# An encoder trunk's gated MLP: where the chained weight additions and the sums of activations stand in VectorE's order

## The chip, the cores and the metric

The kernel runs on one core of one Trainium2 chip. The metric is the device time of one execution in microseconds (us), the median of the runs shown. The engines are called as the profile calls them: PE (TensorE's matmuls) and PEld (its weight loads), DVE (VectorE), ACT (ScalarE), POOL (GpSimd) and SP (SyncE, which here only issues DMAs).

## The reference

Two encoder layers over 256 positions of width 2048, in float32. Each layer is a mixer (layer 0: pooling and grouped-query attention; layer 1: a bidirectional mLSTM) followed by a gated MLP, and the change touches the MLP alone:

```python
def conv_ffn(x, w_up, conv_w, conv_b, w_down):
    u = x @ w_up                       # 2048 -> 2 * 5632
    up = jnp.pad(u, ((0, 0), (1, 1), (0, 0)))
    c = conv_w.astype(u.dtype)
    u = c[0] * up[:, :-2] + c[1] * up[:, 1:-1] + c[2] * up[:, 2:] + conv_b.astype(u.dtype)
    gate, val = jnp.split(u, 2, axis=-1)
    return (jax.nn.silu(gate) * val) @ w_down    # 5632 -> 2048

for layer in range(DEPTH):             # DEPTH = 2
    ...
    x = x + mixed
    x = x + conv_ffn(rms_norm(x, norm_ffn[layer]), w_up[layer], conv_w[layer], conv_b[layer], w_down[layer])
```

## The kernel before, in words

**Precision and the weight stream.** A float32 product is made of three matmuls: every operand is split into a high part (a copy rounded to the type fp32r) and a low part (the operand less its high part), and high by high, high by low and low by high are added up in PSUM. The weights come as a stream of chunks of 128 x 1024 float32 (512 KB), in the order in which PE uses them (class `Stream`). SP loads a chunk into one of six buffers `w`, five chunks ahead. `split` then makes its two parts in `hl` (four buffers): ACT copies the high part (L127), DVE subtracts to get the low part (L128). It is called two chunks ahead of the chunk that PE is on: when PE's instructions for chunk i are written down, chunk i + 2 is split.

**What sets the order.** PE's instructions run in the order written. Those of the other engines are ordered when the program is built, by a planner with a timeline of its own: an instruction may be put ahead of earlier written ones where the plan says that its inputs are there. On the chip each engine then takes its instructions in that fixed order and waits where an input is late. Two means bind the planner: a dependence without a wait (it fixes the order of two instructions of one engine), and `keep_in_program_order`, which puts an instruction behind the one that was last written down for its engine. Work that is to be written down between matmuls is a generator in the queue of `Weave`: PE's loops call `tick` with an estimate of the time that they took, and when a task's time has come its next step is written down; `yield 1.2` asks for 1.2 us until the next step; `until` runs the tasks on until a condition holds.

**The MLP.** The 44 pairs of hidden tiles (128 gate channels with their 128 value channels) are worked off in slabs of 4, 8, 8, 8, 8, 8 (`FCH`). `up(c, f, gt, i)` makes one hidden tile of slab c: 64 matmuls over four chunks (PSUM tile `up`), then the row norm, the convolution, SiLU and the product on ACT and DVE (L419 to L992). Two neighbouring hidden tiles are a pair j, and their float32 results lie in one tile `s` of `quads`. The down-projection of a slab runs while the next slab's tiles are made. Most of it is made by blocks of two by two (two hidden tiles by two halves of the positions by two column blocks) with seven products in place of eight, which needs sums of weight blocks and sums of activation blocks. For each pair j of a slab and each half h of the output columns there is a unit A (four products into PSUM tiles `pp`, two chunks) and a unit B (three products, a chunk and a half).

**The sums of weights.** For h = 0 they are made ahead of time by DMAs in DRAM (`premix`). For h = 1 they are made on the way. The first chunk of unit A is a `Sum`: SP loads one summand into a buffer `sum` (three buffers) and POOL issues a DMA that adds the other (L112, L113). The second chunk is a `Chain`: it is loaded plainly, and then DVE adds the first half of the sum to its first half (L123), and that to its second half (L124), before it is split. So the four chunks of two units A are Sum, Chain, Sum, Chain.

**The sums of activations.** `combine(c, j)` makes four sums of the blocks of pair j: DVE L998 (two subtractions in one instruction), L999 and L1000, then ACT's copies (L1004) and DVE's subtractions (L1005) split them into `s3` (three sums, read by units A; one buffer for each j) and `s1` (read by units B; two buffers for each j).

**Rows.** `_ffn_plan` writes the order. A row is one hidden tile of slab c and, behind it, what it carries of slab c - 1. Where a slab's both halves are made by seven products (slabs 2 to 4 of layer 0, 1 to 4 of layer 1, seven in all), the eight rows of the next slab carry: rows 0 and 1 units A of h = 1 (pairs 0 and 1, then 2 and 3), rows 2 and 3 units B of h = 1, rows 4 and 5 units A of h = 0, rows 6 and 7 units B of h = 0. Behind a finished group of units its PSUM tiles are added into `x` or `acc` by four steps of `drain` (L1061), spread over the next row. The `mix` entry of pair j of slab c stands behind row max(2j + 1, last row that reads the old `s3` of j): rows 4, 4, 5 and 7 in these slabs.

Of the kernel before, what the change touches and what calls it, by code (L numbers as in the profile page):

```python
# [9 lines left out]
F32 = mybir.dt.float32  # L10
F32R = mybir.dt.float32r
# [5 lines left out]
P = 128  # L17
# [15 lines left out]
FCH = [4, 8, 8, 8, 8, 8]  # L33
# [4 lines left out]
WARM = 5  # L38
ATT_PARTS = [[4 + h for h in range(8)], [0, 1, 2, 3], [4 + h for h in range(8, 12)]]
ML_PARTS = [list(range(12)), list(range(12, 16))]  # L40

NG = 4 * KT
NB = D // 512
# [22 lines left out]
class Sum:  # L66


    def __init__(self, one, other):
        self.one, self.other = one, other  # L70
# [15 lines left out]
class Stream:  # L86


    def __init__(self, nc, wpool, spool, srcs, load_ahead, split_ahead):
        self.nc, self.wpool, self.spool, self.srcs = nc, wpool, spool, srcs  # L90
        self.la, self.sa = load_ahead, split_ahead
        self.w, self.hl = {}, {}
        self.n_load = self.n_split = self.at = 0

    def load(self, pieces=1):
# [20 lines left out]
    def split(self, then=None):  # L116
        i = self.n_split
        w, n, width = self.w.pop(i)
        if isinstance(self.srcs[i], Sum):
            self.sum = w  # L120
        elif isinstance(self.srcs[i], Chain):
            half = CH * P // 2
            self.nc.vector.tensor_add(w[:, :half], w[:, :half], self.sum[:, :half])  # L123
            self.nc.vector.tensor_add(w[:, half:], w[:, half:], w[:, :half])  # L124
        hl = self.spool.tile([P, 2, CH * P], F32R, tag="hl", name=f"hl{i}")
        for c in range(0, width, n):
            (self.nc.vector.tensor_copy if i + c == 0 else self.nc.scalar.copy)(hl[:, 0, c : c + n], w[:, c : c + n])  # L127
            self.nc.vector.tensor_sub(hl[:, 1, c : c + n], w[:, c : c + n], hl[:, 0, c : c + n].bitcast(F32))  # L128
            then and then(c // n)
        self.hl[i] = hl  # L130
        self.n_split += 1
# [76 lines left out]
def trunk(ctx: ExitStack, tc: tile.TileContext, gx, xT, xn, call, catt, cml, weights, mixes, out):  # L208
    nc = tc.nc
# [8 lines left out]
    wp = pool("wraw", 6)  # L218
# [8 lines left out]
    gcol = cp.tile([P, NG], F32, tag="gcol", name="gcol")  # L227
    a_x = actp.tile([P, KT, S], F32, tag="B1", name="xT")
    x = xp.tile([P, 2, D], F32, tag="x", name="x")
    st = Stream(nc, wp, sp, weights, 5, 2)  # L230

    gx0 = actp.tile([P, NG + 2 * S], F32, tag="B0", name="gx0")
    ctx.enter_context(tc.manual_schedule(engines={mybir.EngineType.PE}))
# [11 lines left out]
    wv = Weave()  # L245
# [708 lines left out]
    def ffn_layer(layer, norm, nxt):  # L954
        with ExitStack() as es:
# [16 lines left out]
            def up(c, f, gt, i):  # L972
# [11 lines left out]
                v.tensor_add(y[:, :, 1:S], y[:, :, 1:S], z[:, 0, :, 0 : S - 1])  # L984
                v.tensor_add(y[:, :, 0 : S - 1], y[:, :, 0 : S - 1], z[:, 1, :, 1:S])
                if i % 2 == 0:
                    quads[c, i // 2] = tp.tile([P, 4, P], F32, tag="silu", bufs=3, name=f"s{layer}_{f}")
                s_ = quads[c, i // 2][:, i % 2 * 2 : i % 2 * 2 + 2].rearrange("p a b -> p (a b)")
                a.activation(s_, y[:, 0, :], AF.Silu)
# [1 line left out]
                a.copy(gt[:, i, 0, :], s_)  # L991
                v.tensor_sub(gt[:, i, 1, :], s_, gt[:, i, 0, :].bitcast(F32))  # L992

            def combine(c, j):

                g4 = quads.pop((c, j))
                sf = sm1.tile([P, 512], F32, tag="sq", name=f"sf{layer}_{c}_{j}").rearrange("p (a b) -> p a b", a=4)
                v.tensor_sub(sf[:, 0:2], g4[:, 0::3], g4[:, 1:2].to_broadcast([P, 2, P]))  # L998
                v.tensor_add(sf[:, 2], sf[:, 1], g4[:, 0])  # L999
                v.tensor_sub(sf[:, 3], sf[:, 2], g4[:, 2])  # L1000
                s3 = kp.tile([P, 2, 3, P], F32R, tag=f"s3{j}", name=f"s3{layer}_{c}_{j}")
                s1 = st.sums.tile([P, 2, P], F32R, tag=f"s1{j}", name=f"s1{layer}_{c}_{j}")
                for d, e in ((s3, sf[:, 0:3]), (s1, sf[:, 3])):
                    a.copy(d[:, 0], e)  # L1004
                    v.tensor_sub(d[:, 1], e, d[:, 0].bitcast(F32))  # L1005
                combos[c, j] = s3, s1

            def product(ps, xs, wh, wl, first, last):
                xh, xl = xs
# [5 lines left out]
            def unit(kind, c, h, js):  # L1015
# [3 lines left out]
                if js[0] == 0:  # L1019
                    wv.until(lambda: "busy" not in pss)  # L1020
                    for e in order:
                        pss[e] = psp.tile([P, 512], F32, tag="ps", name=f"pp{layer}_{c}_{h}{e}")
                gt = gts[c]

                def part(j, k, t):
# [118 lines left out]
            for kind, c, i, *j in _ffn_plan(layer):  # L1144
                if kind == "up":
                    if i == 0:
                        gts.append(actp.tile([P, 8, 2, S], F32R, tag=f"B{c % 2}", name=f"g{layer}_{c}"))
                    up(c, f, gts[c], i)
                    f += 1
                elif kind == "down":  # L1150
                    down(c, i)
                elif kind == "two":
                    down_two(c)
                elif kind == "mix":
                    combine(c, i)
                else:
                    unit(kind, c, i, *j)

# [65 lines left out]
def _ffn_plan(layer):  # L1224
# [6 lines left out]
    for c, n in enumerate(FCH):  # L1231
# [5 lines left out]
        else:  # L1237
            slots = [[(kind, c - 1, 1, (j,))] for kind in "AB" for j in range(pairs)]
            for b in range(2 if pairs else 0):
                slots[(b + 1) * pairs // 2 - 1].append(("down", c - 1, b))  # L1240

        busy = {j: k for k, slot in enumerate(slots) for u in slot if u[0] == "A" for j in u[3]}
        for i in range(n):
            seq.append(("up", c, i))
            seq += slots[i] if i < len(slots) else []
            if c < len(FCH) - 1:
                seq += [("mix", c, j) for j in range(n // 2) if i == max(2 * j + 1, busy.get(j, 0))]
    return seq + [("two", len(FCH) - 1, 0)] + [("down", len(FCH) - 1, b) for b in range(2, NB)]


# [154 lines left out]
```

## Time and profile before

| | us |
|---|---|
| median of 3 runs | 2175.67 (2175.55 to 2177.23) |
| the profiled execution | 2172.38 |
| span of its trace | 2170.4 |

| engine | busy us | share of the span |
|---|---|---|
| PE | 2160.9 | 100% |
| PEld | 1845.4 | 85% |
| DVE | 1729.7 | 80% |
| ACT | 1406.7 | 65% |
| POOL | 128.7 | 6% |

The granted clock of PE is 1.00 in all stretches that are shown. The span runs from the first to the last instruction of the program. Busy time is the time in which at least one instruction of the engine was running; a view by windows gives it for a stretch of the span, with the number of instructions in brackets, the granted clock, the mean busy share of the 16 DMA engines and what they moved in GB/s. In a timeline the first column is the start in us from the span's start, the second the time that the line covers, and a bracket at the end names idle time of the engine ahead of the instruction and what ended it. The duration of a single instruction includes its tail, which overlaps the next one's beginning: what an instruction costs its engine is the distance to the next start.

### The profile page before, as it was taken

Reading aid. Unit: us, or ns where it says so; the run is one execution under the profiler, and the core shown is the slowest. Engines: PE = TensorE matmul, PEld = TensorE weight load, DVE = VectorE, ACT = ScalarE, POOL = GpSimd, SP = SyncE. Lnnn points to the kernel's source line nnn. Section 1 sums busy time; section 2 is a strip of 40 time slices with the busy share of each in tenths; the row PEclk is TensorE's granted clock in tenths of the full one; section 3 lists DMA queues with packets and bytes.
Section 4 is the critical chain, followed back from the end, with each engine's and each line's share of the span. In section 5 each row is a group of like instructions: output and inputs, shape, how many; then the busy total and the mean of one; then the engine's idle time right before and its main releaser. Section 6 shows DMA issues by size and latency. Waiting matters only on the chain.

```text
span 2170.4 us, 31559 instructions
## 1 busy us (share of the span) xinstructions
PE 2160.9 (100%) x11424; PEld 1845.4 (85%) x11424; DVE 1729.7 (80%) x2428; ACT 1406.7 (65%) x2200; POOL 128.7 (6%) x160
## 2 busy tenths in 40 slices
PE   9999999999999999999999999999999999999999
PEld 7888888888888888889888888888888888888887
DVE  7686678887988888976777676667888898988896
ACT  7665576766677767666554554457676777776763
POOL 0011010000000000000000010110000000000000
PEclk9999999999999999999999999999999999999999
DMA  9668988787988877757688888998978787887774
GB/s 326 220 204 255 287 247 263 231 268 243 293 272 278 281 247 234 253 193 226 203 250 248 252 243 243 276 274 249 270 214 283 253 272 248 264 266 242 233 252 163
DMA packets 157790, 543.72 MB, mean 251 GB/s; under 512 B 17498, under 2 KB 19842, under 8 KB 157634
## 3 DMA queue, kind: packets, MB, share of 16 engines
q1 hardware_dynamic: 129056, 460.10, 61.1%
q0 software_dynamic: 17440, 48.51, 13.5%
q10 hardware_dynamic: 11138, 33.11, 4.6%
q8 instruction: 89, 1.46, 0.3%
q14 instruction: 67, 0.55, 0.1%
HBM read 539.50 MB, written 60.86 MB: 277 GB/s over the span
## 4 chain that ended last, share of the span: by engine, by line
PE 92%; DVE 4%; DMA 3%; issue 1%; ACT 1%; DVEq 0%; ACTq 0%; POOLq 0%
PE up L256 40%; PE pp L256 11%; PE op L256 8%; PE dn L256 6%; PE mv L256 4%; PE mq L256 4%; PE mk L256 4%; PE mo L256 4%; PE qproj L256 3%; DVE hl L128 2%; DMA w<-in_dn 1%; PE kproj L256 1%; PE vproj L256 1%; DMA sum<-in_dn 1%; PE pool L256 1%
## 5 line engine op out<-in xcount | busy, mean ns | idle before, releaser
L128 DVE TENSOR_TENSOR hl<-w,hl 128x1024 fp32r<-128x1024 f32 (+2 forms) x836 | 1002.8, 1211 | 223.3 <-ACT hl L127 220.6
L127 ACT CAST hl<-w 128x1024 fp32r<-128x1024 f32 (+2 forms) x835 | 857.2, 1043 | 450.5 <-PE up L256 134.3
L256 PE MATMUL up<-xx,hl 128*128 128x512 f32 (+1 forms) x5632 | 996.6, 337 | 3.2 <-DVE hl L128 3.0
L256 PEld LDWEIGHTS up<-xx,hl 128*128 128x128 f32 x5632 | 865.9, 188 | 137.9 <-DVE hl L128 7.9
L256 PE MATMUL pp<-hl,s 128*128 128x512 f32 x768 | 193.2, 393 | 0.4 <-DVE hl L128 0.4
L256 PEld LDWEIGHTS pp<-hl,s 128*128 128x128 f32 x768 | 141.3, 188 | 30.2 <-DVE hl L128 1.6
L256 PE MATMUL pp<-hl,g 128*128 128x512 f32 x576 | 147.9, 391 | 0.0
L419 ACT COPY tb_up<-up 128x512 f32<-128x512 f32 x88 | 51.6, 586 | 113.0 <-PE up L256 112.8
L256 PEld LDWEIGHTS pp<-hl,g 128*128 128x128 f32 x576 | 105.4, 188 | 20.7
L256 PE MATMUL dn<-hl,g 128*128 128x512 f32 x528 | 122.7, 390 | 0.0
L256 PEld LDWEIGHTS dn<-hl,g 128*128 128x128 f32 x528 | 98.7, 188 | 20.3
L983 ACT ACTIVATE y<-tb_up,cst 128x256 f32<-128x256 f32 x176 | 103.6, 589 | 0.0
L984 DVE TENSOR_TENSOR y<-y,z 128x510 f32<-128x510 f32 x88 | 60.5, 688 | 50.2 <-ACT y L983 50.2
L981 ACT ACTIVATE z<-tb_up,cst 128x256 f32<-128x256 f32 x176 | 88.4, 502 | 7.9 <-DVE tb_up L976 6.4
L256 PE MATMUL mk<-xx,hl 128*128 128x512 f32 (+1 forms) x512 | 92.1, 337 | 0.0
L256 PE MATMUL mq<-xx,hl 128*128 128x512 f32 (+1 forms) x512 | 92.1, 337 | 0.0
L256 PE MATMUL mv<-hl,xx 128*128 128x512 f32 (+2 forms) x480 | 91.7, 350 | 0.0
L256 PE MATMUL op<-hl,cat 128*128 128x512 f32 x384 | 91.6, 393 | 0.0
L420 DVE TENSOR_TENSOR tb_up<-up,tb_up 128x512 f32<-128x512 f32 x88 | 60.6, 688 | 38.4 <-ACT tb_up L419 38.4
L256 PE MATMUL mo<-hl,xx 128*128 128x512 f32 x384 | 90.5, 391 | 0.0
L256 PE MATMUL op<-hl,mcat 128*128 128x512 f32 x384 | 89.5, 392 | 0.0
L256 PEld LDWEIGHTS mq<-xx,hl 128*128 128x128 f32 x512 | 79.2, 188 | 11.6
(232 smaller groups left out, 2097.0 us busy)
## 6 DMA issues: line engine op xcount, KB each, us to landing
w<-in_up SPq DMA_DIRECT2D x352, 512.0 KB, 4.8
w<-in_dn SPq DMA_DIRECT2D x176, 512.0 KB, 4.5
w<-in_m_in SPq DMA_DIRECT2D x124, 512.0 KB, 5.3
m<-in_dn ACTq DMA_DIRECT2D x56, 512.0 KB, 6.0
w<-m SPq DMA_DIRECT2D x56, 512.0 KB, 4.8
w<-in_a_in SPq DMA_DIRECT2D x46, 512.0 KB, 4.8
sum<-in_dn SPq DMA_DIRECT2D x36, 512.0 KB, 4.9
sum<-in_dn POOLq DMA_DIRECT2D x36, 512.0 KB, 8.9
```

The source lines that it names most:

```text
L127: (self.nc.vector.tensor_copy if i + c == 0 else self.nc.scalar.copy)(hl[:, 0, c : c + n], w[:, c : c + n])
L128: self.nc.vector.tensor_sub(hl[:, 1, c : c + n], w[:, c : c + n], hl[:, 0, c : c + n].bitcast(F32))
L256: last_mm[0] = pe.matmul(out_, lhsT, rhs, start=start, stop=stop, skip_group_check=True)
L419: a.copy(tb, ps[:, :, 1, :])
L420: v.tensor_add(tb, ps[:, :, 0, :], tb)
L981: a.activation(z[:, 0, j, :], u[:, j, :], AF.Copy, scale=cw(tl, 0))
L983: a.activation(y[:, j, :], u[:, j, :], AF.Identity, scale=cw(tl, 1), bias=cw(tl, 3))
L984: v.tensor_add(y[:, :, 1:S], y[:, :, 1:S], z[:, 0, :, 0 : S - 1])
```

## The change

It has two parts, both in the order of work; no instruction's operands or sizes change.

In `Stream`, the first addition of a Chain chunk (L123) gets an order behind the low part of the chunk that stands two places ahead of it in the stream. The order has no wait on a semaphore, as both are on DVE. `lows` holds the two last low parts written down.

`combine` becomes a generator that makes the sums of several pairs one after the other, is queued in `Weave`, and has its DVE instructions pinned behind what was written down for DVE before. A table `MIX` says in which row it is queued: pair 0 of slab c behind row 4 of that slab, pairs 1 and 2 behind row 6, pair 3 behind row 0 of the next slab, the last with a delay of 6.0 us, the others with 0.6 (slab 0, with two pairs: rows 1 and 3). `unit` runs the queue until its pairs' sums are written down, and `up` does so until fewer than three of the tiles `s` are still to be read.

```diff
--- before.py
+++ after.py
@@ -39,6 +39,11 @@
 ATT_PARTS = [[4 + h for h in range(8)], [0, 1, 2, 3], [4 + h for h in range(8, 12)]]
 ML_PARTS = [list(range(12)), list(range(12, 16))]
 
+
+MIX = {(0, 1): [(0, [0])], (0, 3): [(0, [1])]}
+for _c in range(1, len(FCH) - 1):
+    MIX.update({(_c, 4): [(_c, [0])], (_c, 6): [(_c, [1, 2])], (_c + 1, 0): [(_c, [3])]})
+
 NG = 4 * KT
 NB = D // 512
 
@@ -86,10 +91,10 @@
 class Stream:
 
 
-    def __init__(self, nc, wpool, spool, srcs, load_ahead, split_ahead):
-        self.nc, self.wpool, self.spool, self.srcs = nc, wpool, spool, srcs
+    def __init__(self, nc, behind, wpool, spool, srcs, load_ahead, split_ahead):
+        self.nc, self.behind, self.wpool, self.spool, self.srcs = nc, behind, wpool, spool, srcs
         self.la, self.sa = load_ahead, split_ahead
-        self.w, self.hl = {}, {}
+        self.w, self.hl, self.lows = {}, {}, []
         self.n_load = self.n_split = self.at = 0
 
     def load(self, pieces=1):
@@ -120,12 +125,14 @@
             self.sum = w
         elif isinstance(self.srcs[i], Chain):
             half = CH * P // 2
-            self.nc.vector.tensor_add(w[:, :half], w[:, :half], self.sum[:, :half])
+            self.behind(self.nc.vector.tensor_add(w[:, :half], w[:, :half], self.sum[:, :half]), self.lows[0])
             self.nc.vector.tensor_add(w[:, half:], w[:, half:], w[:, :half])
         hl = self.spool.tile([P, 2, CH * P], F32R, tag="hl", name=f"hl{i}")
         for c in range(0, width, n):
             (self.nc.vector.tensor_copy if i + c == 0 else self.nc.scalar.copy)(hl[:, 0, c : c + n], w[:, c : c + n])
-            self.nc.vector.tensor_sub(hl[:, 1, c : c + n], w[:, c : c + n], hl[:, 0, c : c + n].bitcast(F32))
+            low = self.nc.vector.tensor_sub(
+                hl[:, 1, c : c + n], w[:, c : c + n], hl[:, 0, c : c + n].bitcast(F32))
+            self.lows = self.lows[-1:] + [low]
             then and then(c // n)
         self.hl[i] = hl
         self.n_split += 1
@@ -227,7 +234,13 @@
     gcol = cp.tile([P, NG], F32, tag="gcol", name="gcol")
     a_x = actp.tile([P, KT, S], F32, tag="B1", name="xT")
     x = xp.tile([P, 2, D], F32, tag="x", name="x")
-    st = Stream(nc, wp, sp, weights, 5, 2)
+    order = mybir.DependencyInfo(mybir.DependencyClass.NoSync, mybir.DependencyReason.SCHED_ONLY)
+
+    def behind(ins, other):
+
+        tc.add_manual_dep(ins.ins, other.ins.name, order, reason="order")
+
+    st = Stream(nc, behind, wp, sp, weights, 5, 2)
 
     gx0 = actp.tile([P, NG + 2 * S], F32, tag="B0", name="gx0")
     ctx.enter_context(tc.manual_schedule(engines={mybir.EngineType.PE}))
@@ -984,6 +997,7 @@
                 v.tensor_add(y[:, :, 1:S], y[:, :, 1:S], z[:, 0, :, 0 : S - 1])
                 v.tensor_add(y[:, :, 0 : S - 1], y[:, :, 0 : S - 1], z[:, 1, :, 1:S])
                 if i % 2 == 0:
+                    wv.until(lambda: sum(e < len(FCH) - 1 for e, _ in quads) < 3)
                     quads[c, i // 2] = tp.tile([P, 4, P], F32, tag="silu", bufs=3, name=f"s{layer}_{f}")
                 s_ = quads[c, i // 2][:, i % 2 * 2 : i % 2 * 2 + 2].rearrange("p a b -> p (a b)")
                 a.activation(s_, y[:, 0, :], AF.Silu)
@@ -991,19 +1005,28 @@
                 a.copy(gt[:, i, 0, :], s_)
                 v.tensor_sub(gt[:, i, 1, :], s_, gt[:, i, 0, :].bitcast(F32))
 
-            def combine(c, j):
-
-                g4 = quads.pop((c, j))
-                sf = sm1.tile([P, 512], F32, tag="sq", name=f"sf{layer}_{c}_{j}").rearrange("p (a b) -> p a b", a=4)
-                v.tensor_sub(sf[:, 0:2], g4[:, 0::3], g4[:, 1:2].to_broadcast([P, 2, P]))
-                v.tensor_add(sf[:, 2], sf[:, 1], g4[:, 0])
-                v.tensor_sub(sf[:, 3], sf[:, 2], g4[:, 2])
-                s3 = kp.tile([P, 2, 3, P], F32R, tag=f"s3{j}", name=f"s3{layer}_{c}_{j}")
-                s1 = st.sums.tile([P, 2, P], F32R, tag=f"s1{j}", name=f"s1{layer}_{c}_{j}")
-                for d, e in ((s3, sf[:, 0:3]), (s1, sf[:, 3])):
-                    a.copy(d[:, 0], e)
-                    v.tensor_sub(d[:, 1], e, d[:, 0].bitcast(F32))
-                combos[c, j] = s3, s1
+            def combine(c, js):
+
+                pin = tc.keep_in_program_order
+                for j in js:
+                    g4 = quads[c, j]
+                    sf = sm1.tile([P, 512], F32, tag="sq", name=f"sf{layer}_{c}_{j}").rearrange(
+                        "p (a b) -> p a b", a=4)
+                    pin(v.tensor_sub(sf[:, 0:2], g4[:, 0::3], g4[:, 1:2].to_broadcast([P, 2, P])))
+                    yield 0.9
+                    pin(v.tensor_add(sf[:, 2], sf[:, 1], g4[:, 0]))
+                    pin(v.tensor_sub(sf[:, 3], sf[:, 2], g4[:, 2]))
+                    yield 1.2
+                    s3 = kp.tile([P, 2, 3, P], F32R, tag=f"s3{j}", name=f"s3{layer}_{c}_{j}")
+                    s1 = st.sums.tile([P, 2, P], F32R, tag=f"s1{j}", name=f"s1{layer}_{c}_{j}")
+                    for d, e in ((s3, sf[:, 0:3]), (s1, sf[:, 3])):
+                        a.copy(d[:, 0], e)
+                    yield 1.2
+                    for d, e in ((s3, sf[:, 0:3]), (s1, sf[:, 3])):
+                        pin(v.tensor_sub(d[:, 1], e, d[:, 0].bitcast(F32)))
+                        yield 0.6
+                    del quads[c, j]
+                    combos[c, j] = s3, s1
 
             def product(ps, xs, wh, wl, first, last):
                 xh, xl = xs
@@ -1020,6 +1043,7 @@
                     wv.until(lambda: "busy" not in pss)
                     for e in order:
                         pss[e] = psp.tile([P, 512], F32, tag="ps", name=f"pp{layer}_{c}_{h}{e}")
+                wv.until(lambda: all((c, j) in combos for j in js))
                 gt = gts[c]
 
                 def part(j, k, t):
@@ -1152,7 +1176,7 @@
                 elif kind == "two":
                     down_two(c)
                 elif kind == "mix":
-                    combine(c, i)
+                    wv.add(combine(c, i), 6.0 if 3 in i else 0.6)
                 else:
                     unit(kind, c, i, *j)
 
@@ -1238,13 +1262,10 @@
             slots = [[(kind, c - 1, 1, (j,))] for kind in "AB" for j in range(pairs)]
             for b in range(2 if pairs else 0):
                 slots[(b + 1) * pairs // 2 - 1].append(("down", c - 1, b))
-
-        busy = {j: k for k, slot in enumerate(slots) for u in slot if u[0] == "A" for j in u[3]}
         for i in range(n):
             seq.append(("up", c, i))
             seq += slots[i] if i < len(slots) else []
-            if c < len(FCH) - 1:
-                seq += [("mix", c, j) for j in range(n // 2) if i == max(2 * j + 1, busy.get(j, 0))]
+            seq += [("mix", *e) for e in MIX.get((c, i), ())]
     return seq + [("two", len(FCH) - 1, 0)] + [("down", len(FCH) - 1, b) for b in range(2, NB)]
```

## The prediction

> **What bounds the kernel now.** I read the page's first part, then the waits of PE, then windows cut where PE starts a new slab.
>
> ```profile
> PE 2160.9 (100%) x11424; PEld 1845.4 (85%) x11424; DVE 1729.7 (80%) x2428; ACT 1406.7 (65%) x2200; POOL 128.7 (6%) x160
> PE up L256 <- DVE hl L128: 3.0, 6, 0.7
> PE pp L256 <- DVE hl L128: 0.4, 1, 0.4
> ```
>
> PE sets the time, and no matmul is added or taken away. So the change can only give back what PE loses by waiting. In the MLP that is seven waits, all for the low part of a weight chunk (L128). What a wait shows as idle is less than it costs, because the two matmuls before the one that waits are stretched too. So I take the cost from lengths: one window for each of the seven slabs' rows, and windows of single rows of one of them.
>
> ```profile
> 542.84:671.25 128.41, 128.00 (x681) 109.13 (x680) 113.52 (x152) 94.78 (x144) 6.71 (x8) 1.00 0.86 281
> 671.25:801.36 130.11, 128.87 (x681) 108.90 (x680) 115.42 (x154) 92.45 (x141) 6.78 (x8) 1.00 0.86 273
> 801.36:929.46 128.10, 128.06 (x682) 109.44 (x682) 115.00 (x143) 91.23 (x137) 1.19 (x2) 1.00 0.72 238
> 1609.20:1737.06 127.86, 127.81 (x682) 109.23 (x681) 109.31 (x145) 94.36 (x145) 3.44 (x4) 1.00 0.81 261
> 1737.06:1866.46 129.40, 128.34 (x681) 109.09 (x681) 114.93 (x154) 92.65 (x140) 3.41 (x4) 1.00 0.81 260
> 1866.46:1994.91 128.45, 127.84 (x681) 109.22 (x680) 115.78 (x154) 93.12 (x141) 3.44 (x4) 1.00 0.81 262
> 1994.91:2123.23 128.32, 128.07 (x682) 109.44 (x681) 115.17 (x143) 91.31 (x137) 0.85 (x1) 1.00 0.72 238
> sum 900.65, PE 896.99 PEld 764.46 DVE 799.12 ACT 649.90 POOL 25.83; mean PE 128.14 PEld 109.21 DVE 114.16 ACT 92.84 POOL 3.69
> ```
>
> The columns are the stretch, its length, then busy PE, PEld, DVE, ACT and POOL. The rows of the slab from 1866.46 on, with the last row before it:
>
> ```profile
> 1851.22:1866.46 15.24, 15.24 (x83) 13.11 (x82) 11.67 (x17) 11.07 (x17) 0.00 (x0) 1.00 0.74 240
> 1866.46:1883.97 17.51, 16.90 (x89) 14.16 (x88) 17.51 (x24) 12.18 (x18) 0.85 (x1) 1.00 0.70 220
> 1883.97:1900.62 16.65, 16.65 (x89) 14.18 (x88) 16.07 (x23) 12.83 (x22) 1.73 (x2) 1.00 1.01 328
> 1900.62:1915.86 15.24, 15.24 (x83) 13.10 (x82) 14.39 (x21) 10.50 (x15) 0.87 (x1) 1.00 1.00 313
> 1947.76:1964.43 16.67, 16.67 (x89) 14.23 (x88) 13.82 (x20) 12.71 (x22) 0.00 (x0) 1.00 0.73 250
> ```
>
> These are row 7 of the slab before, then rows 0, 1, 2 and 5. A row with units A takes 16.67 us where nothing waits, one with units B 15.24, so eight rows take 4 x 16.67 + 4 x 15.24 = 127.64 and seven slabs 893.48. They took 900.65. **7.17 us, 0.33% of the time, is all that can come back there.** Row 0 alone lost 17.51 - 16.67 = 0.84, with DVE busy throughout; in row 7 just before it DVE had 15.24 - 11.67 = 3.57 us free. The timeline of DVE across that border says why (the last two lines are PE's):
>
> ```profile
> 1860.85 1.23 DVE L128 TENSOR_TENSOR hl<-w,hl 128x1024 fp32r<-128x1024 f32 x1 [1.22 <-ACT hl L127]
> 1864.00 0.69 DVE L123 TENSOR_TENSOR w<-w,sum 128x512 f32<-128x512 f32 x1 [1.59 <-DMA w<-in_dn]
> 1864.61 0.68 DVE L420 TENSOR_TENSOR tb_up<-up,tb_up 128x512 f32<-128x512 f32 x1
> 1865.21 0.68 DVE L124 TENSOR_TENSOR w<-w 128x512 f32<-128x512 f32 x1
> 1866.41 1.22 DVE L128 TENSOR_TENSOR hl<-w,hl 128x1024 fp32r<-128x1024 f32 x1
> 1866.46 0.39 PE L256 MATMUL up<-xx,hl 128*128 128x512 f32 x1
> 1867.68 10.96 PE L256 MATMUL up<-xx,hl 128*128 128x256 f32 x62 [0.61 <-DVE hl L128]
> ```
>
> The low part of row 0's first chunk starts at 1866.41, just when PE wants it. Before it stands the addition of a Chain chunk that PE needs five chunks later. DVE waited 1.59 us for that chunk's load, with everything behind it, and then spent two additions of 0.60 (start to start). The low part would have been ready some 2.8 us sooner.
>
> **The change, part by part.** *Chained additions.* There are 36 Chain chunks, and L123's waits for loads are
>
> ```profile
> L123 DVE TENSOR_TENSOR w<-w,sum x36: 677/692/694, 298.3 to 2015.9; 128x512 f32<-128x512 f32 x36
> DVE w L123 <- DMA w<-in_dn: 26.2, 17, 2.9
> DVE w L123 <- DMA sum<-in_dn: 4.2, 2, 2.3
> ```
>
> 30.4 us of DVE in 19 waits. By the new order the first addition of the Chain in place 6 stands behind the low part of place 4, and that of place 8 behind place 6. It then runs after the low parts which PE needs first, and its load, asked for five chunks ahead, has had three more chunks' time (2.8 us each) to land. So I count these waits as gone. Nothing is added to DVE's work. Two costs are new. If the additions stand next to each other, the second must wait for the first's end, 0.68, instead of starting at 0.60. And ACT's copy of the chunk, about 1.0, must come between them and the chunk's low part; the low part of the chunk between (1.14) covers it. Without that cover DVE idles 1.0 for each Chain, 2.0 in each of rows 0 and 1.
>
> The dependent neighbours in the trace cost a bit more than the tail:
>
> ```profile
> 1789.50 0.68 DVE L984 TENSOR_TENSOR y<-y,z 128x510 f32<-128x510 f32 x1
> 1790.21 0.69 DVE L985 TENSOR_TENSOR y<-y,z 128x510 f32<-128x510 f32 x1
> ```
>
> 0.71 from start to start against 0.60, so 0.11 a Chain, 0.22 a row: covered by the lead that the waits give back. The Trainium skill ("VectorE: DVE Perf Modes", The DRAIN you can't avoid) says that a semaphore between chained DVE operations costs nothing extra, since the next one waits for an empty pipe anyway; by it the 0.11 would be 0. This trace disagrees for additions, by that 0.71.
>
> How much of the 7.17 hangs on these waits? Not all of it:
>
> ```profile
> 721.43:737.59 16.16, 15.63 (x83) 13.14 (x84) 14.31 (x19) 13.36 (x23) 0.00 (x0) 1.00 0.85 311
> 1786.77:1802.73 15.96, 15.59 (x84) 13.11 (x83) 14.07 (x19) 12.38 (x21) 0.00 (x0) 1.00 0.76 261
> 1782.39 1.05 ACT L127 CAST hl<-w 128x1024 fp32r<-128x1024 f32 x1 [2.73 <-DMA w<-in_dn]
> ```
>
> Two rows 3 lost 0.92 and 0.72. There ACT itself waits for a load: in rows 1 and 2 the DMA engines are full (1.01 and 1.00 above), with the sums' loads and additions in them. Leaving out 0.4 for the row before the first of them, that is 2.0 us of late loads, and 7.17 - 2.0 = **5.2 us for the early additions**. For the late loads the bounds are 0 (the DMA share stays) and 2.0 (DVE, less behind, frees its buffers earlier); I take 0.7, nearer to nothing, because the same bytes must move.
>
> *The sums of activations.* 36 pairs, each with three DVE sums, two ACT copies and two DVE low parts; no DMA is issued.
>
> ```profile
> L1005 DVE TENSOR_TENSOR s<-sf,s x72: 279/420/554, 295.2 to 2018.7; 128x384 fp32r<-128x384 f32 x36, 128x128 fp32r<-128x128 f32 x36
> L998 DVE TENSOR_TENSOR sf<-s x36: 408/417/425, 291.5 to 2008.2; 128x256 f32<-128x256 f32 x36
> L999 DVE TENSOR_TENSOR sf<-sf,s x36: 278/283/291, 292.2 to 2010.3; 128x128 f32<-128x128 f32 x36
> ```
>
> With L1000 like L999 a pair costs DVE at most 0.42 + 0.28 + 0.28 + 0.84 = 1.8 us, or 1.4 with the tails of 0.08 taken off. The work is the same; its place is not. Pair 0 goes into row 5, pairs 1 and 2 into row 7. Row 5 has 16.67 - 13.82 = 2.85 us free and gives up pair 1. Row 7 takes about 2.8, less what it held of pair 2, and gives up the wait and the two additions; with 3.57 free it holds that, and nothing waits for these pairs before the next slab. The tile `s` of pair 1 is kept until row 7, with pairs 0 and 2 beside it three in all, and pair 0's is free again in row 5, before row 6 asks for one. Slab 0's pairs keep their rows, and `until` issues nothing. Cost: 0; without that room, up to 2.8 in row 7 of seven slabs. Pair 3 is the tight one. Its sums are now written down 6 us into row 1, behind the low part of the first of the four chunks of the units A that follow, and its own low parts behind that of the second. PE reads its `s3` with the third:
>
> ```profile
> 1888.67 0.55 DVE L1005 TENSOR_TENSOR s<-sf,s 128x384 fp32r<-128x384 f32 x1
> 1894.56 1.22 DVE L128 TENSOR_TENSOR hl<-sum,hl 128x1024 fp32r<-128x1024 f32 x1
> 1897.88 2.22 PE L256 MATMUL pp<-hl,s 128*128 128x512 f32 x9
> ```
>
> Before, `s3` was there at 1889.2, 8.7 us ahead of its use at 1897.88. The low part at 1894.56 is that of the third chunk, so that of the second ends at about 1894.6; behind it `s3` comes at some 1895.5: 2.4 us to spare. Queued behind these on DVE are the low parts of the third and fourth chunks, and PE waits for those next. Bounds: 0, and the whole 1.4 in each of seven rows, 9.9. As the lead in that row is about 2 us (the low part of 1894.56 ends 2.1 before its use) and grows by what row 0 no longer wastes, I take 0.1 a slab, 0.7.
>
> **Sum:** -5.2 - 0.7 + 0.7 = -5.2 us on the profiled execution's 2172.38, so 2167.2. The median of the runs is 3.29 above it; by the same difference 2175.67 - 5.2 = **2170.5**. For this way of going alone: -7.2 to -3.0, 2168.5 to 2172.7.
>
> **The rivals.** (a) *The wait moves into pair 3's sums: slower.* The pinned instructions meet a DVE that has no lead; the late chunks of row 1, or `s3` itself, come 1.4 us late in seven rows: +9.9 - 5.2 = +4.7, 2180.4. It decides from 5.2 / 7 = 0.74 a row. For it: in row 1 DVE is busy 16.07 of 16.65. Against: pair 3's sums stood in rows 0 and 1 before too, so the two rows' work is the same but for the additions from row 7. (b) *Row 0 stays short of DVE.* Its work is at least the 17.51 of now, plus the two additions that stood before it, against 16.67; if the lead that row 7 leaves is used up, about half of the 5.2 is lost again: 2173.1. Against: row 7's free time and the 1.59 make a lead of some 3 us, more than the 2.0 that row 0 lacks. (c) *The change does nothing to the stalls:* the planner puts other early work there, and loads decide: 2175.5. Against: in the row 0 shown DVE's only wait for a load is L123's, and the order forbids that place to it.
>
> **How the numbers follow.** Forecast 0.60, (a) 0.17, (b) 0.15, (c) 0.08. A difference of 0.2%, 4.35 us, is about what a measurement can tell from none. The forecast is beyond it in five cases of six (0.50), and the tail of (b) adds 0.02: faster 0.52. Slower is (a) and a little of (c): 0.18. The rest, 0.30, lies within. The range goes from the cap, 7.2 off (2168.5), up to 2178.5: it holds (b), (c) and the milder part of (a).
>
> **What would show it.** Right: no wait of L123 for a DMA; slabs of 127.6 to 128.0 us; row 0 at 16.7, and first chunks of a slab no longer late. Rows 3 with late loads may stay. Wrong: PE waits for ACT or DVE of `s` (L1004, L1005) or for L128 in row 1; a longer wait of L128 for ACT's copy than before in rows 0 and 1; slabs over 128.7 us.

## The result, and the profile after

| | before | after |
|---|---|---|
| median of the runs, us | 2175.66 (2175.55 to 2177.23) | 2189.3 (2188.71 to 2190.35) |
| the profiled execution, us | 2172.38 | 2188.71 |
| span of its trace, us | 2170.4 | 2186.6 |

The changed kernel takes 1.0062 times as long [1.0044, 1.0079]: **13.6 us slower, where 5.2 us faster was forecast**. The time lies outside the range. The granted clock is 1.00 in all stretches that this section shows, as before.

The first part of the page after, to be held against that of before (PE 2160.9 us, DVE 1729.7):

```profile
PE 2165.9 (99%) x11424; PEld 1845.7 (84%) x11424; DVE 1735.1 (79%) x2428; ACT 1404.8 (64%) x2200; POOL 128.5 (6%) x160
```

The counts of instructions are the same. Two lines of the waits of PE stand in the place of the seven waits for L128 (columns: us in total, times, longest; the low part is now L133 and ACT's high part L132):

```profile
PE pp L269 <- DVE hl L133: 11.1, 12, 1.1
PE pp L269 <- ACT hl L132: 3.2, 11, 0.6
```

PE no longer waits before `up`, at the head of a slab, but before `pp`, in the units. The first addition of a Chain chunk (now L128) has no wait for a load left in 36 instructions, where 30.4 us stood; its row among the groups of instructions of the kernel after (busy us, mean ns, idle time before it):

```profile
L128 DVE TENSOR_TENSOR w<-w,sum 128x512 f32<-128x512 f32 x36 | 24.6, 684 | 0.0
```

So the wait that the change was to remove is removed, and the time went elsewhere. The windows of the same seven slabs (the stretch, its length, then busy PE, PEld, DVE, ACT, POOL), with three of them left out, of 131.57, 131.83 and 131.59 us:

```profile
542.96:673.64 130.68, 128.76 (x682) 109.14 (x680) 114.57 (x151) 93.93 (x146) 6.71 (x8) 1.00 0.87 278
...
1616.54:1744.53 127.99, 127.93 (x682) 109.30 (x681) 111.85 (x148) 93.97 (x147) 3.43 (x4) 1.00 0.82 260
...
1876.12:2007.68 131.56, 128.99 (x681) 109.12 (x680) 116.28 (x153) 92.39 (x141) 3.44 (x4) 1.00 0.79 256
2007.68:2139.52 131.84, 129.26 (x682) 109.33 (x681) 116.17 (x145) 91.55 (x138) 0.85 (x1) 1.00 0.72 232
sum 917.06, PE 902.14 PEld 764.45 DVE 807.40 ACT 648.39 POOL 25.81; mean PE 128.88 PEld 109.21 DVE 115.34 ACT 92.63 POOL 3.69
```

917.06 - 900.65 = 16.41 us, all of the 16.33 by which the two profiled executions differ. Six slabs lose 3.0 to 4.2 us against the 127.64 of rows without a wait; the fourth loses 0.35. Cut by rows, around the slab that the prediction showed, and with row 0 of the fourth slab as the last line:

```profile
1860.88:1876.12 15.24, 15.24 (x84) 13.10 (x82) 13.66 (x23) 11.27 (x20) 0.00 (x0) 1.00 0.71 243
1876.12:1896.75 20.63, 18.06 (x89) 14.00 (x88) 18.80 (x26) 14.12 (x22) 0.85 (x1) 1.00 0.68 200
1896.75:1913.39 16.64, 16.64 (x89) 14.23 (x88) 15.73 (x21) 10.69 (x17) 1.72 (x2) 1.00 0.92 298
1616.54:1633.21 16.67, 16.67 (x90) 14.24 (x89) 15.27 (x22) 12.93 (x22) 0.87 (x1) 1.00 0.77 214
```

In this slab the whole loss lies in row 0: 20.63 - 16.67 = 3.96. Row 7 ahead of it and row 1 behind it run without a wait. Four more slabs have the same row 0 (20.62 to 20.64); the first of the seven loses its 3.0 us in rows 0 to 2 (18.53, 17.43 and 15.67). Row 0 of the fourth slab, under the same order, loses nothing. DVE had 15.27 us of work there: the four steps of `drain` (L1085, 0.60 each), which stand in the row shown, are not in it. (The 18.80 of the row shown were counted over a row that is 3.96 us longer.) Inside row 0, first PE (start, us covered, and in brackets idle time and what ended it):

```profile
1876.12 11.30 PE L269 MATMUL up<-xx,hl 128*128 128x512 f32 x64
1887.25 1.55 PE L269 MATMUL pp<-hl,s 128*128 128x512 f32 x6
1889.05 0.50 PE L269 MATMUL pp<-hl,s 128*128 128x512 f32 x1 [0.24 <-ACT hl L132]
1890.68 0.74 PE L269 MATMUL pp<-hl,s 128*128 128x512 f32 x2 [1.13 <-DVE hl L133]
1894.15 0.49 PE L269 MATMUL pp<-hl,s 128*128 128x512 f32 x1 [0.29 <-ACT hl L132]
1895.48 0.74 PE L269 MATMUL pp<-hl,s 128*128 128x512 f32 x2 [0.84 <-DVE hl L133]
```

Each of the two units A takes six matmuls of its Sum chunk, then waits for both parts of its Chain chunk. DVE in the same row:

```profile
1881.60 1.22 DVE L133 TENSOR_TENSOR hl<-w,hl 128x1024 fp32r<-128x1024 f32 x1
1882.73 0.69 DVE L128 TENSOR_TENSOR w<-w,sum 128x512 f32<-128x512 f32 x1
1883.33 1.22 DVE L133 TENSOR_TENSOR hl<-sum,hl 128x1024 fp32r<-128x1024 f32 x1
1884.47 0.68 DVE L1085 TENSOR_TENSOR x<-x,pp 128x512 f32<-128x512 f32 x1
1885.07 0.42 DVE L1004 TENSOR_TENSOR s<-s,y 128x256 f32<-128x256 f32 x1
1885.40 0.68 DVE L1085 TENSOR_TENSOR x<-x,pp 128x512 f32<-128x512 f32 x1
1886.00 0.68 DVE L129 TENSOR_TENSOR w<-w 128x512 f32<-128x512 f32 x1
1886.60 0.42 DVE L1006 TENSOR_TENSOR g<-s,g 128x256 fp32r<-128x256 f32 x1
1888.07 0.69 DVE L433 TENSOR_TENSOR tb_up<-up,tb_up 128x512 f32<-128x512 f32 x1 [1.05 <-ACT tb_up L432]
1888.80 0.69 DVE L989 TENSOR_TENSOR tb_up<-tb_up,R 128x512 f32<-128x512 f32 x1
1889.41 1.22 DVE L133 TENSOR_TENSOR hl<-w,hl 128x1024 fp32r<-128x1024 f32 x1
1890.54 0.68 DVE L128 TENSOR_TENSOR w<-w,sum 128x512 f32<-128x512 f32 x1
```

The first line is the low part of the chunk two places ahead of the first Chain. Right behind it, at the first moment that the order allows, the Chain's first addition starts (1882.73). The chunk's own low part ends at 1889.41 + 1.22 = 1890.63, 7.9 us later. PE's unit began at 1887.25 and wants that low part with its eighth matmul. A matmul takes 0.231 there (in the kernel with distance four, below, nine fill the time from 1875.43 to 1877.51), so it is due at 1887.25 + 7 x 0.231 = 1888.87, **6.1 us after 1882.73**. The second Chain's first addition, tied to the first one's low part, starts at 1890.54, and the same is repeated. In the kernel before, these additions stood at 1864.00 and 1865.21, in row 7's idle time, ahead of row 0. Row 7 lost them and yet its DVE time grew from 11.67 to 13.66: the sums of activations stand there now.

### The profile page after: what moved, and what is told of

Same layout as the page of the kernel before. It is cut to its first block, busy times and chain, and to the rows that moved or that the text cites. A ratio compares the mean times of both kernels' runs of the same rounds, so it can differ in the third digit from the quotient of the medians.

```text
span 2186.6 us, 31567 instructions
## 1 busy us (share of the span) xinstructions
PE 2165.9 (99%) x11424; PEld 1845.7 (84%) x11424; DVE 1735.1 (79%) x2428; ACT 1404.8 (64%) x2200; POOL 128.5 (6%) x160
## 4 chain that ended last, share of the span: by engine, by line
PE 96%; DVE 3%; ACT 1%; issue 0%; ACTq 0%; DVEq 0%
PE up L269 44%; PE pp L269 12%; PE op L269 8%; PE dn L269 5%; PE mv L269 4%; PE mq L269 4%; PE mk L269 4%; PE mo L269 4%; PE qproj L269 3%; DVE hl L133 2%; PE kproj L269 1%; PE vproj L269 1%; PE pool L269 1%; PE qk L269 1%; PE av L269 1%; PE end L269 0%
## 5 line engine op out<-in xcount | busy, mean ns | idle before, releaser
L133 DVE TENSOR_TENSOR hl<-w,hl 128x1024 fp32r<-128x1024 f32 (+2 forms) x836 | 999.1, 1211 | 234.9 <-ACT hl L132 232.8
L132 ACT CAST hl<-w 128x1024 fp32r<-128x1024 f32 (+2 forms) x835 | 854.2, 1043 | 469.8 <-PE up L269 137.4
L269 PE MATMUL pp<-hl,s 128*128 128x512 f32 x768 | 200.7, 397 | 14.8 <-DVE hl L133 11.1
L269 PEld LDWEIGHTS dn<-hl,g 128*128 128x128 f32 x528 | 98.7, 188 | 20.3
```

The source lines that it names most:

```text
L133: low = self.nc.vector.tensor_sub(hl[:, 1, c : c + n], w[:, c : c + n], hl[:, 0, c : c + n].bitcast(F32))
L269: last_mm[0] = pe.matmul(out_, lhsT, rhs, start=start, stop=stop, skip_group_check=True)
```

## The experiments

In all of them "order" means the dependence of a Chain's first addition on an earlier low part, and its distance is how many places in the stream that low part stands ahead. Each ratio is against the kernel before, measured beside it on the same chip; three groups of four kernels had 2175.54, 2175.81 and 2175.09 us there.

### Which part of the change, and which distance

**The order alone** (`edge2`): the kernel before with the changed `Stream`, without the new `combine`, `MIX` and `until`.

> The order of the chained additions alone, the sums of activations as before. Theory O (the order is the cause: in row 0 DVE has no free time, and between the low part two places ahead and the Chain chunk's own low part lie some 8 us of DVE and ACT work where PE allows 6): slower than before by most of the 13.6 us, 2184 to 2190, with PE waiting in rows 0 at the second chunk of each unit A. Rival S (the sums of activations in row 7 take the time in which DVE made its lead): about 5 us faster than before, 2170, no waits in row 0. Rival Q (ACT's copy of the finished hidden tile, which waits for PE, stands ahead of the Chain's copy; in this kernel's order it stands behind it at the first Chain): half of the loss, 2180 to 2183, the first unit's waits gone.

**The sums alone** (`mix`): the changed kernel without the order.

```diff
-            self.behind(self.nc.vector.tensor_add(w[:, :half], w[:, :half], self.sum[:, :half]), self.lows[0])
+            self.nc.vector.tensor_add(w[:, :half], w[:, :half], self.sum[:, :half])
```

> The sums of activations step by step in their new rows alone, the additions free for the planner as before. Theory O: within 3 us of before, 2173 to 2178, with L128's waits for loads (the first addition) as before. Rival S: slower by most of the 13.6 us, 2184 to 2190. Rival Q: as theory O.

**The order alone at distance four** (`edge4`; `both4` is the changed kernel with the same line):

```diff
-            self.lows = self.lows[-1:] + [low]
+            self.lows = self.lows[-3:] + [low]
```

> The order alone, but behind the low part four places ahead instead of two; the sums of activations as before. Theory O: the additions come two low parts earlier, next to each other, and still not ahead of the first chunk of a row, so both the early additions' waits and the late Chain are gone: 3 to 6 us faster than before, 2169.7 to 2172.7. Rival S: the same as for two places, 2170. Rival Q: as theory O, since the Chain's copy stands ahead of the tile's copy.

> The changed kernel with four places instead of two. Theory O: faster than before, 2168 to 2173; the changed sums cost nothing or give a little. Rival S: still slower than before by 8 us or more. Rival Q: faster than before, since here the Chain's copy stands ahead of the tile's copy.

| kernel | us | ratio to before |
|---|---|---|
| order, distance two | 2188.77 | 1.0063 [1.0046, 1.0079] |
| sums alone | 2180.71 | 1.0027 [1.0017, 1.0037] |
| order, distance four | 2168.46 | 0.9970 [0.9959, 0.9981] |
| sums and order, distance four | 2168.98 | 0.9973 [0.9963, 0.9983] |

The order at distance two alone makes a loss of the same size (13.2 us), and the same order at distance four gains 7.1 us. Between the two lie 20.3 us, and as many between the kernels with the sums (2189.3 and 2168.98). O's times held for the order at distance two and for both parts at distance four. The order at distance four came out below all that was expected, and the sums alone between the ranges of O and S.

The loss of the order alone is not made of the same waits as that of the changed kernel, though, nor of a wait in each unit as O had it. With the order alone at distance two, row 0 of the same slab begins at 1876.14. PE in it, and from DVE the low part of the first Chain and the first addition of the second:

```profile
1887.28 2.24 PE L264 MATMUL pp<-hl,s 128*128 128x512 f32 x9
...
1893.06 0.50 PE L264 MATMUL pp<-hl,s 128*128 128x512 f32 x1 [1.36 <-ACT hl L127]
1894.32 0.74 PE L264 MATMUL pp<-hl,s 128*128 128x512 f32 x2 [0.76 <-DVE hl L128]
```

```profile
1887.25 1.23 DVE L128 TENSOR_TENSOR hl<-w,hl 128x1024 fp32r<-128x1024 f32 x1
1888.40 0.68 DVE L123 TENSOR_TENSOR w<-w,sum 128x512 f32<-128x512 f32 x1
```

The first unit does not wait: the first Chain's low part ends at 1888.48, 6.3 us after its first addition at 1882.14, and is due at 1887.28 + 7 x 0.231 = 1888.90, 6.8 after it. (ACT's copy of that chunk stands ahead of its copy of the hidden tile here, as Q expected; Q's time, half of the loss, did not come.) The second Chain's first addition starts behind that low part, at 1888.40; its unit begins at 1890.05, so its low part is due at 1891.67, 3.3 us later. It ends at 1894.26, 5.9 us later. The row takes 19.45 us, 2.8 more than 16.67.

And not all of the 13.2 us is waiting. Right behind the waits in three of the six slabs the granted clock of PE is lower, 0.87 in this window by the column before the last two; no other profile of this document has such a stretch in its slabs:

```profile
1762.90:1776.32 13.42, 13.42 (x69) 11.54 (x67) 11.64 (x15) 8.37 (x14) 0.86 (x1) 0.87 1.00 307
```

The 64 matmuls of `up` in the three rows that follow take 12.24, 12.75 and 12.82 us where they take 11.30 elsewhere; with the matmuls just ahead of them that adds up to some 4.8 us. Over the whole span the clock is 0.998 (0.997 or 0.998 in each execution of this kernel). Other slabs have the same waits (1.36 and 0.76 from 805.28 on) and no such stretch; why it comes is not shown.

The slabs of the profiled execution with the order alone at distance four, and then DVE at its row 0, which begins at 1864.30:

```profile
sum 897.16, PE 895.70 PEld 765.25 DVE 800.74 ACT 648.02 POOL 25.83; mean PE 127.96 PEld 109.32 DVE 114.39 ACT 92.57 POOL 3.69
```

```profile
1862.34 2.35 DVE L128 TENSOR_TENSOR hl<-w,hl 128x1024 fp32r<-128x1024 f32 x2
1864.62 0.68 DVE L123 TENSOR_TENSOR w<-w,sum 128x512 f32<-128x512 f32 x1
1865.34 0.69 DVE L124 TENSOR_TENSOR w<-w 128x512 f32<-128x512 f32 x1
...
1873.55 1.22 DVE L128 TENSOR_TENSOR hl<-w,hl 128x1024 fp32r<-128x1024 f32 x1
```

PE in the same row:

```profile
1864.30 11.30 PE L264 MATMUL up<-xx,hl 128*128 128x512 f32 x64
1875.43 2.24 PE L264 MATMUL pp<-hl,s 128*128 128x512 f32 x9
1877.51 0.85 PE L264 MATMUL pp<-hl,g 128*128 128x512 f32 x3
```

The additions stand behind the low parts of row 0's first two chunks, so these are no longer late, but still at the border of row 7; the Chain's low part is done at 1874.77, before the units of this row begin at 1875.43.

The sums alone cost 5.2 us, and the waits of PE in that kernel name the place:

```profile
PE pp L269 <- DVE s L1026: 7.4, 6, 1.6
```

```profile
1902.68 0.62 PE L269 MATMUL pp<-hl,s 128*128 128x512 f32 x2
1904.14 1.88 PE L269 MATMUL pp<-hl,s 128*128 128x512 f32 x7 [0.83 <-DVE s L1026]
```

```profile
1903.54 0.55 DVE L1026 TENSOR_TENSOR s<-sf,s 128x384 fp32r<-128x384 f32 x1
```

(the waits, PE in row 1, DVE there). Pair 3's `s3` is ready at 1904.09, when PE has been at its unit since 1902.68. In the changed kernel no such wait is left, and with distance four there is one, of 1.6 us; so the parts' losses do not add up (13.2 + 5.2 against 13.6).

### Where the order bites: the first Chain of two, or the second

Two causes were open for distance two. L: the first Chain is late, as DVE has no room in row 0. K: the order is a chain, since the second Chain's additions wait for the first one's low part. One kernel puts the first Chain of each row at distance two and the second at four (`near_far`), another the reverse (`far_near`); two more put all at three (`edge3`) and at five (`edge5`). The edit of the first of them, against the order alone at distance two:

```diff
-            self.behind(..., self.lows[0])
+            self.behind(..., self.lows[-2 if self.chains % 2 == 0 else -4])
+            self.chains += 1
...
-            self.lows = self.lows[-1:] + [low]
+            self.lows = self.lows[-3:] + [low]
```

> The order alone; the first Chain of each two behind the low part two places ahead, the second four ahead. Theory K (the loss is the second Chain's: two places ahead of it stands the first Chain's own low part, so its additions, copy and low part start only when the first is done): the waits at the second units go, 2168 to 2173. Rival L (any addition that is not made before row 0's full DVE load costs): the first Chain is still in it, 2178 to 2186.

> The order alone; the first Chain four places ahead, the second two. Theory K: the first Chain is done earlier, by the trace with four ahead at 1874.8 against a use of the second at 1879.6; from the second's addition to its low part's end the trace with two ahead needs 5.9 us, so it is late by about 1 us in six slabs: 2173 to 2179. Rival L: only one of two Chains is in the full load, 2175 to 2180. A time under 2171 would speak against both.

> The order alone, three places ahead: the first Chain behind the low part of the row's third chunk, the second behind the Sum between them. Theory K: the second no longer waits for the first, so most of the 13 us is gone: 2169 to 2176. Rival L: the additions are still within row 0's load, only 1.1 us earlier: 2180 to 2187.

> The order alone, five places ahead. Both theories: near the time of four ahead, 2167 to 2172; the first addition may again meet a load that has not landed (up to 1 us of DVE in some rows), which would bring it towards the kernel before.

| order, distance of first and second Chain | us | ratio to before |
|---|---|---|
| 2 and 4 | 2178.49 | 1.0011 [1.0001, 1.0021] |
| 4 and 2 | 2168.49 | 0.9966 [0.9954, 0.9978] |
| 3 and 3 | 2177.29 | 1.0002 [0.9990, 1.0013] |
| 5 and 5 | 2172.67 | 0.9983 [0.9971, 0.9994] |

Neither theory held as it was put. With 2 and 4 the time lies in L's range; with 4 and 2 it lies under the 2171 that was to speak against both; at three it lies between the two ranges, and at five just above the one that both gave. What the runs show is that the second Chain's place matters through the first. Where the first is early, the second at distance two costs nothing by the medians (2168.49 against 2168.46 with both at four; its row 0 takes 17.07 us in five slabs, 0.40 more than 16.67). With the first at two and the second at four PE waits at the first Chain (0.24 and 0.76 in the slab shown, and 0.28 in the second unit), and that costs some 10 us (2178.49). With both at two it is some 20 (2188.77), but this is not the same wait with another added: in the trace above PE waits at the second Chain alone, and some 4.8 us are the lower clock. The first Chain need not be late for PE to make the second late; it is enough that it is ready just when PE wants it. Distance three comes out like 2 and 4, in its rows 0 too (18.76 and 18.77). At five the first addition goes ahead of the low part of row 0's second chunk, and part of what was lost before comes back, the waits for loads and waits of PE before `up`:

```profile
PE up L264 <- DVE hl L128: 2.2, 3, 1.6
DVE w L123 <- DMA w<-in_dn: 14.2, 8, 3.9
```

### ACT's queue, and pair 3

In the kernel with 2 and 4, ACT stood before the late Chain as follows:

```profile
1881.93 0.59 ACT L429 COPY tb_up<-up 128x512 f32<-128x512 f32 x1 [1.54 <-PE up L266]
1882.41 1.06 ACT L129 CAST hl<-w 128x1024 fp32r<-128x1024 f32 x1
```

DVE had made the second additions of both Chains by then:

```profile
1880.46 1.29 DVE L126 TENSOR_TENSOR w<-w 128x512 f32<-128x512 f32 x2
```

The Chain's high copy stands behind the copy of the hidden tile, which waits for PE's last matmul of `up`. The additions had ended by 1880.46 + 1.29 = 1881.75, so the copy began at least 0.66 late. Cause Q: this order on ACT makes the loss. Two kernels put the tile's copy behind the high copy of the chunk that was split last, where that is a Chain; one is made from 2 and 4 (`near_far_q`), one from the changed kernel (`after_q`):

```diff
...
+            self.high = high if isinstance(self.srcs[i], Chain) else None
...
-        a.copy(tb, ps[:, :, 1, :])
+        copy = a.copy(tb, ps[:, :, 1, :])
+        st.high and behind(copy, st.high)
```

> As the kernel with the first Chain two places ahead and the second four, and besides ACT's copy of a finished hidden tile stands behind the high part of the Chain chunk that was split last. Theory Q (in that kernel ACT waited 1.5 us for PE to finish the row, with the first Chain's copy, whose inputs were there, behind it): the waits of 0.5, 1.0 and 0.55 us in each of six slabs go, 2166 to 2171. Rival L (DVE's load in row 0 is what makes the first Chain late): the waits stay, 2175 to 2180.

> The changed kernel with that one order on ACT. Theory Q with K (both Chains two places ahead: the first Chain's wait goes with the order on ACT, the second's stays because it starts behind the first's low part): 1.9 us in five slabs come back and up to 0.6 are lost again at the second Chain, 2180 to 2187. If Q alone made the whole loss: 2168 to 2173. If Q has no part: 2188 to 2190.

The first gave 2175.57 us, 1.0003 [0.9993, 1.0012], the second 2190.93, 1.0076 [1.0061, 1.0091]. Where only the first Chain is late, Q is worth some 2 of the 10 us (2.7 over the kernel before in one group of runs, 0.5 in the other), and PE still waits for the low part (row 0 takes 18.17 us in place of 18.77). In the changed kernel it is worth nothing. PE in the row 0 that was shown above, which begins there at 1878.33:

```profile
1889.46 2.60 PE L270 MATMUL pp<-hl,s 128*128 128x512 f32 x9
...
1893.67 1.44 PE L270 MATMUL pp<-hl,s 128*128 128x512 f32 x5 [0.68 <-DVE hl L134]
1895.40 0.50 PE L270 MATMUL pp<-hl,s 128*128 128x512 f32 x1 [0.30 <-ACT hl L132]
1896.66 0.72 PE L270 MATMUL pp<-hl,s 128*128 128x512 f32 x2 [0.76 <-DVE hl L134]
```

The first unit runs without the waits of 0.24 and 1.13; in the second a wait of 0.68 for its Sum chunk is new, and its Chain waits as before. Row 0 takes 19.59 us, 1.04 less than in the changed kernel, but row 1 behind it, which had no wait there, now waits 0.69 for the low part of its second Chain and takes 17.63, 0.96 more than 16.67. Neither expectation held as a whole; Q is a part of the one loss and not the cause of the other.

**Pair 3 queued at once**: all entries of `MIX` with the delay 0.6, in the kernel with the sums alone (`mix_early3`) and in the one with both parts at distance four (`both4_early3`).

```diff
-                    wv.add(combine(c, i), 6.0 if 3 in i else 0.6)
+                    wv.add(combine(c, i), 0.6)
```

> The sums of activations alone, in their new rows, with pair 3 queued 0.6 us into row 1 instead of 6.0. Theory A (the 5 us of that part are PE's waits for pair 3's sums, 7.4 us in six slabs): these waits go and the time comes to 2172 to 2177. Rival S (the loss is the 3 us of DVE work put into row 7): it stays at 2179 to 2182.

> The changed kernel with four places instead of two and pair 3 queued 0.6 us into row 1. Theory A: the one wait left for pair 3's sums, 1.6 us in slab 3 of layer 0, goes: 2166 to 2168. Rival S: no change against 2169.

The sums alone now take 2174.12 us, 0.9994 [0.9985, 1.0003]: no wait for `s` is left, and the 5.2 us are gone. Both parts with distance four take 2168.43, 0.9969 [0.9958, 0.9980]. Two waits of PE are left in that kernel, of 1.2 us (tile `wps`) and 0.8 us (tile `ptr`), neither in the seven slabs:

```profile
sum 894.20, PE 894.14 PEld 765.39 DVE 802.60 ACT 649.27 POOL 25.72; mean PE 127.73 PEld 109.34 DVE 114.66 ACT 92.75 POOL 3.67
```

894.20 is 0.72 above the 893.48 of slabs without a wait, so in these slabs nothing more is to be had from waits. It beats both kernels; from the simplest version that does so, the order at distance four alone, the runs don't tell it apart.

## Why the prediction was wrong

**What the early additions cost: right.** The cap of 7.17 us, the place (row 0's first chunks, held up by L123) and the means (a place behind other low parts) hold. In the changed kernel no wait of L123 for a load is left; with the order alone at distance four five are, 7.8 us of the 30.4. That looser order brings back 7.1 us by the medians and 3.5 by the slabs of the profiled executions (900.65 - 897.16); the forecast was 5.2. The late loads, of which I took 0.7 of 2.0, were not tested by themselves; with both parts at distance four and pair 3 queued at once, 6.45 of the 7.17 are back (900.65 - 894.20), the rows 3 among them. (One window was 0.08 too long: the second of these rows ended at 1802.65, and lost 0.64, not 0.72; the 2.0 stands.)

**The step that failed** is in "Chained additions": "It then runs after the low parts which PE needs first", "Nothing is added to DVE's work", and the claim that one low part covers ACT's copy. The additions do run after those low parts, but then their own chunk is the next that PE needs, and that date was never worked out. For DVE as a whole the work is the same; for row 0 it is not. The additions left row 7, which had 3.57 us free, for a row that I had myself quoted with DVE busy for all of 17.51 us. Both dates were to be had from the trace of before: PE's from its matmuls in row 0, DVE's from the drains, the tile's product and the splits of that row. For the first Chain the profile after shows them as 7.9 us of work and waits against 6.1. The addition, its neighbour, the copy and the low part themselves need only 0.60 + 0.68 + 1.06 + 1.22 = 3.6; what the planner put between them takes the rest. In the order alone the planner put less there, 6.3 against 6.8, and PE did not wait at this chunk. Row 0 of the fourth slab, without the four drains, is the case where my sum would have been right.

**The second term that was missing** is the chain from Chain to Chain. I wrote that the order puts place 8 behind place 6 and took that for a gain of time for the load. It also gives the second Chain no earlier start than the first one's low part: 3.3 us before its own date in the order alone, where it took 5.9, and 3.0 in the changed kernel (from 1890.54 to 1891.95 + 7 x 0.231 = 1893.57). Even the 3.6 us of its own four instructions don't fit into that. With the second at distance four instead, some 10 of the 20 us between the distances go; of those 10, some 4.8 are the lower clock that the profile of the order alone shows behind its waits.

**Rival (b)**, row 0 short of DVE, named the right place with the right objection for it, and was mis-sized: I let it take back half of the 5.2 us that were won. A stall there isn't bounded by what the change gains. Some 20 us lie between the two distances, four times the gain. The lead of some 3 us that I set against it did not exist for these chunks: a lead counts only for an instruction that may run early, and the order forbade that.

**Rival (a)**, pair 3's sums, is real where the sums stand alone: they cost 5.2 us with `s3` late, where I had priced that wait at up to 9.9 (+4.7 after the gain of 5.2) and taken 0.7 for my sum. The margin of 2.4 us for `s3` was wrong by over 3. I had reckoned it behind the second chunk's low part of before; pinned in the order written, it came behind everything written down for DVE in that row. In the changed kernel the wait does not show. DVE may catch up there while PE stalls in row 0, but that isn't needed for it: with both parts at distance four, without a stall in row 0, five of the six waits are gone too. In the slab shown `s3` is ready 12.6 us into that row 1, where its unit begins at 13.9; with the sums alone it is ready at 15.3. DVE waits 0.84 for a load in front of a Chain's addition in that row there, and not here; whether that makes the difference no run separates.

**Rows 5 and 7 with pairs 0 to 2** cost nothing, as forecast: row 7 takes 15.24 with 13.66 of DVE in it. **Signs:** I had asked for PE waiting for L128 in row 1; it came in row 0, whose units I had not watched. The first sign of being right, no wait of L123 for a DMA, came true in a kernel that lost: it shows that the wait went, and nothing of what replaced it.

## What to carry to other kernels

An order that keeps work from running too early is also a date before which it can't run: work out, for the row into which the work moves, its earliest start, all that its engine has to do from there and the date at which it is needed, and compare. A row where an engine has no free time takes nothing more, however much the same engine has free next door. If the order ties each piece of work to the one before it, the date of each hangs on that of its predecessor: here a first Chain that came just in time already made the second late. A looser distance (here four in place of two) kept the gain, and PE waits in none of its rows 0.

## What was not expected of the hardware

A wait cost more than the trace shows as idle: in row 0 after, the brackets add up to 0.24 + 1.13 + 0.29 + 0.84 = 2.50 us, and the row is 3.96 longer. ACT takes its instructions strictly in turn in these traces: in the kernel with distances 2 and 4 a copy whose input was there waited 0.66 us behind one that waited for PE. The Trainium skill ("Perfetto Trace Analysis", Tensor Engine Instruction) says the same of ACT and DVE, that both are strict FIFO, and that trace agrees. And dependent additions on DVE again lay 0.72 apart (1864.62 to 1865.34 at distance four) where independent ones lie 0.60 apart (1885.40 to 1886.00 after). The Trainium skill ("VectorE: DVE Perf Modes", The DRAIN you can't avoid) holds a chained operation's semaphore to cost nothing extra, from a measurement of copies; these rows show 0.12. Of that, 0.08 is the first addition's tail (0.68 long, where the next independent one starts after 0.60) and 0.04 lies behind its end; what of it the semaphore makes is not shown.
